# Splitting weights of later stages during the feed-forward stages, with the parts kept in DRAM

## The chip, the cores and the metric

One core of a Trainium2 chip runs the whole program. The metric is the device time of one execution in microseconds (us), and the median of several runs counts. The engines are named as the profile names them: PE multiplies matrices, PEld loads its weights, DVE, ACT and POOL do the elementwise work, and SP issues all the DMA transfers of this kernel.

## The reference, cut to what matters

The program computes a first block of two layers (each: feed-forward 1, a mix of three attentions, feed-forward 2) and a second block (memory attention, forgetting attention "fox", linear recurrence "lru", stick-breaking attention "sb", then a convolved feed-forward), all in float32, for 512 tokens of width 1024.

```python
def hybrid_layer(x, ...):
    x = x + 0.5 * swiglu(rmsnorm(x, ffn1_norm), ffn1_w_gate, ffn1_w_up, ffn1_w_down)
    h = rmsnorm(x, mix_norm) @ w_in
    ...
    x = x + jnp.concatenate([o_a, o_b, o_c], axis=-1) @ w_out
    x = x + 0.5 * swiglu(rmsnorm(x, ffn2_norm), ffn2_w_gate, ffn2_w_up, ffn2_w_down)
    return x
```

`o_b` attends only to the 128 keys with the highest scores of each query; `o_a` and `o_c` are dense. Block 2 projects the normalized state with one wide matrix, runs the four branches, gates them and adds them up.

## The kernel before, in words

**Number format.** PE multiplies in a format (fp32r) that holds only the upper part of a float32. Each weight tile is therefore split into a high part `wh` and a rest `wl`, the activations likewise, and `mm3` (lines 308 to 310) makes three matmuls of them: high by high, high by rest, rest by high. The product of a 128 x 1024 weight tile and 512 tokens is 8 x 3 = 24 matmuls of 128 x 512.

**A weight tile's way.** `weights` (line 283) takes a tile `raw` (two buffers) and loads it by a DMA of SP (line 289). ACT copies it into `wh` (line 293); DVE, for every other tile POOL, subtracts and writes `wl` (line 296). `wh` and `wl` have four buffers each. So a tile costs one load of up to 512 KB, one ACT and one DVE or POOL instruction.

**Stages.** `ffn` (line 392) goes over 22 hidden blocks in two halves (12 and 10): gate and up projections of a block, the gating by ACT, POOL and DVE, a split of the result; then 8 output blocks per half, each with two down tiles of 768 or 640 columns. `mix` (line 594) projects, ropes, and runs 16 heads in the order of `MIX_PLAN`: heads A, C, B; scores and the search for the 128 best keys (`topk`, lines 661 and 662 on DVE) belong to heads B. In `head` (line 463) DVE adds the bias and finds the maximum (473), ACT takes the exponential (478), POOL scales the row (480), PE transposes (517), ACT and DVE split the transposed weights (302, 303), PE multiplies with the values (527). At the end the head outputs are split into `hs` (302, 303) and multiplied with `wo`. `block2` runs `memkv`, then `mem`, `fox`, `lru`, `sb`.

**Order.** The code is written in program order; a scheduler of the language lays every instruction into a fixed queue of its engine ahead of the run, from its own estimate of when operands and buffers come free. Each engine works through its queue in order, SP too: a transfer that waits for a buffer holds up those behind it. Small transfers are in SP's queue as well: the swaps of rope (569, 570) and the copies that stack queries and keys (440, 449).

**Names used.** `st` is a tile of 128 x 1280 with two buffers that holds softmax rows in the attention stages; `nt` is a two-part tile of 128 x 512 with two buffers, used for queries and keys. Neither is used in `ffn` before the change.

## Time and profile before

| | |
|---|---|
| median of 3 runs | 3550.11 us (3547.43 to 3553.41) |
| the profiled execution, its own time | 3547.53 us |
| span in the profile (first to last instruction) | 3545.1 us |
| PE busy | 3452.3 us, 97% |
| DVE, ACT, POOL busy | 1959.9, 1432.8, 1534.5 us (55%, 40%, 43%) |
| mean granted PE clock | 0.988 |
| DMA moved | 397.60 MB, mean 112 GB/s |

Busy time of an engine is the time in which at least one of its instructions ran; PE's is modelled and overlaps from one matmul to the next. The granted clock is the share of PE's full clock: 1.00 is 2.4 GHz, and a stretch at 0.66 was for two thirds of it at 1.2 GHz.

### The profile page before, as it was taken

What the parts mean: (1) busy time and instruction counts of PE and PEld (TensorE: products, weight loads), DVE (VectorE), ACT (ScalarE), POOL (GpSimd) and SP (SyncE); (2) the same over time, 40 slices, a digit from 0 to 9 for tenths busy, and PEclk for the clock granted to TensorE, in tenths of its full rate; (3) what the DMA queues carried; (4) which work ended last, traced back from release to release, by engine and by line L of the source; (5) the groups of instructions that cost most, each with busy time, mean ns of one, the idle gap of its engine ahead of it and who ended that gap; (6) DMA issues with size and microseconds to landing.
All of it is one profiled execution on the core that took longest, in us unless ns stands there. A gap on an engine that the chain in (4) does not pass through costs nothing.

```text
span 3545.1 us, 45441 instructions
## 1 busy us (share of the span) xinstructions
PE 3452.3 (97%) x16648; PEld 2882.8 (81%) x16648; DVE 1959.9 (55%) x3210; ACT 1432.8 (40%) x2366; POOL 1534.5 (43%) x1224
## 2 busy tenths in 40 slices
PE   8999999999999999999999999999999999999999
PEld 7888778788888888777888888888777788888887
DVE  5434697653445344796643465358536655657363
ACT  4223455532333233465422344346525445533222
POOL 3333346342424232446333343258635557635342
PEclk9999999999999999999999999999999999999999
DMA  3333433333233333334433243344532454442332
GB/s 134 91 106 107 128 99 112 109 99 97 94 98 95 95 101 124 110 90 118 122 93 108 85 129 107 104 132 137 152 122 90 157 160 129 128 143 95 95 101 89
DMA packets 141261, 397.60 MB, mean 112 GB/s; under 512 B 18144, under 2 KB 21600, under 8 KB 141040
## 3 DMA queue, kind: packets, MB, share of 16 engines
q1 hardware_dynamic: 141040, 394.71, 36.6%
q8 instruction: 132, 2.16, 0.3%
q14 instruction: 89, 0.73, 0.1%
HBM read 327.24 MB, written 20.48 MB: 98 GB/s over the span
## 4 chain that ended last, share of the span: by engine, by line
PE 47%; DVE 5%; POOL 2%; ACT 2%; issue 2%; DMA 1%; SPq 0%; POOLq 0%; ACTq 0%; DVEq 0%
PE pd L308 10%; PE pd L309 10%; PE pd L310 10%; PE pa L308 4%; PE pa L309 4%; PE pa L310 4%; PE po L527 1%; PE pt L517 1%; DVE wl L296 1%; PE pa L456 1%; POOL st L503 0%; DMA qk<-nt 0%; DVE st L1087 0%; POOL f L499 0%; ACT wh L293 0%
## 5 line engine op out<-in xcount | busy, mean ns | idle before, releaser
L296 POOL TENSOR_TENSOR wl<-raw,wh 128x1024 fp32r<-128x1024 f32 (+3 forms) x315 | 718.0, 2279 | 1135.7 <-ACT wh L293 1112.7
L293 ACT ACTIVATE wh<-raw 128x1024 fp32r<-128x1024 f32 (+3 forms) x631 | 609.5, 967 | 1323.7 <-PE pd L309 841.2
L308 PE MATMUL pd<-hs,wh 128*128 128x512 f32 (+1 forms) x2008 | 791.2, 395 | 19.7 <-ACT wh L293 7.8
L309 PE MATMUL pd<-hs,wh 128*128 128x512 f32 (+1 forms) x2008 | 790.9, 394 | 5.8 <-DVE hs L303 5.4
L310 PE MATMUL pd<-hs,wl 128*128 128x512 f32 (+1 forms) x2008 | 790.5, 394 | 2.4 <-DVE wl L296 1.7
L296 DVE TENSOR_TENSOR wl<-raw,wh 128x1024 fp32r<-128x1024 f32 (+3 forms) x316 | 383.4, 1213 | 232.8 <-ACT wh L293 226.2
L308 PEld LDWEIGHTS pd<-hs,wh 128*128 128x128 f32 (+1 forms) x2008 | 378.4, 189 | 100.7 <-ACT wh L293 14.1
L309 PEld LDWEIGHTS pd<-hs,wh 128*128 128x128 f32 (+1 forms) x2008 | 379.2, 189 | 84.8 <-DVE hs L303 6.2
L310 PEld LDWEIGHTS pd<-hs,wl 128*128 128x128 f32 (+1 forms) x2008 | 378.6, 189 | 85.2 <-DVE wl L296 4.6
L308 PE MATMUL pa<-hs,wh 128*128 128x512 f32 x896 | 349.3, 390 | 0.0
L309 PE MATMUL pa<-hs,wh 128*128 128x512 f32 x896 | 349.2, 390 | 0.0
L310 PE MATMUL pa<-hs,wl 128*128 128x512 f32 x896 | 349.0, 389 | 0.0
L408 POOL TENSOR_TENSOR f<-f,g 128x512 f32<-128x512 f32 x88 | 145.0, 1650 | 279.9 <-ACT g L406 273.5
L407 DVE TENSOR_TENSOR f<-pa,rb 128x512 f32<-128x512 f32 x88 | 60.8, 691 | 272.4 <-PE pa L310 272.4
L310 PEld LDWEIGHTS pa<-hs,wl 128*128 128x128 f32 x896 | 168.4, 188 | 35.0
L309 PEld LDWEIGHTS pa<-hs,wh 128*128 128x128 f32 x896 | 168.2, 188 | 34.9
L308 PEld LDWEIGHTS pa<-hs,wh 128*128 128x128 f32 x896 | 168.4, 188 | 34.6
L480 POOL TENSOR_SCALAR st<-st,ta 128x128 f32<-128x128 f32 x192 | 111.7, 584 | 107.1 <-DVE ta L479 101.0
L303 DVE TENSOR_TENSOR pt<-pt 128x384 fp32r<-128x384 f32 (+1 forms) x200 | 116.8, 597 | 50.0 <-ACT pt L302 48.7
L308 PE MATMUL pd<-ys,wh 128*128 128x512 f32 x362 | 142.3, 393 | 0.2 <-DVE f L741 0.2
L310 PE MATMUL pd<-ys,wl 128*128 128x512 f32 x362 | 141.9, 392 | 0.0
L309 PE MATMUL pd<-ys,wh 128*128 128x512 f32 x362 | 141.8, 392 | 0.0
(385 smaller groups left out, 6468.3 us busy)
## 6 DMA issues: line engine op xcount, KB each, us to landing
raw<-in_wg_dram SPq DMA_DIRECT2D x88, 512.0 KB, 3.5
raw<-in_wu_dram SPq DMA_DIRECT2D x88, 512.0 KB, 3.4
raw<-in_win_dram SPq DMA_DIRECT2D x38, 512.0 KB, 3.5
qk<-nt SPq DMA_DIRECT2D x76, 256.0 KB, 3.9
raw<-in_w2gt_dram SPq DMA_DIRECT2D x32, 512.0 KB, 3.7
raw<-in_w2br_dram SPq DMA_DIRECT2D x32, 512.0 KB, 3.5
qk<-nt SPq DMA_DIRECT2D x108, 128.0 KB, 2.5
raw<-in_wd1a_dram SPq DMA_DIRECT2D x32, 384.0 KB, 3.0
```

The costliest lines, as they stand in the source:

```text
L293: nc.scalar.activation(h[:, :n], raw[:, :n], AF.Copy)
L296: (nc.vector if sub == "v" else nc.gpsimd).tensor_sub(lo[:, :n], raw[:, :n], h[:, :n].bitcast(FT))
L303: (eng or nc.vector).tensor_sub(dst[rows, 1, cols], src, dst[rows, 0, cols].bitcast(FT))
L308: mm(out, wh, xh, start=start, stop=False)
L309: mm(out, wh, xl, start=False, stop=False)
L310: mm(out, wl, xh, start=False, stop=stop)
L407: nc.vector.tensor_mul(u, pu, rb)
L408: nc.gpsimd.tensor_mul(ga, ga, s)
L456: self.nc.tensor.matmul(ps[:, :n], q[:, s, t], k[s][:, x, :n], start=x == 0, stop=x == 1)
L480: nc.gpsimd.tensor_scalar(st[:, c], st[:, c], sm, 0.0, op0=OP.mult, op1=OP.add)
L517: nc.tensor.transpose(pt[:, at + (i - lo) * P:at + (i - lo + 1) * P], st[:, OFF[i] + j * P:OFF[i] + (j + 1) * P], self.ident)
L527: nc.tensor.matmul(po[:, q:q + n], va[:, o:o + P], w[:, x, c:c + n], start=j == 0 and x == 0, stop=j == 2 * g + 1 and x == 1)
```

## The change

During four of the feed-forward stages `prepare` loads tiles of weights that a later stage uses into `st`, splits them in halves of 512 columns into `nt` (ACT copies, DVE subtracts for every other tile, POOL for the rest), and stores both parts into a tile in DRAM. `weights` called with a key loads the two stored parts straight into `wh` and `wl`, with no instruction of ACT, DVE or POOL. The tables: feed-forward 1 of layer 0 prepares 36 tiles of mix 0; feed-forward 2 of layer 0 those of mix 1; feed-forward 1 of layer 1 27 tiles (fox, two of the recurrence); feed-forward 2 of layer 1 40 tiles (recurrence, stick-breaking). That is 139 tiles, in 261 halves. `wo`, the gates and branches of block 2, `mem`, and all feed-forward weights are split as before. Line numbers of the changed kernel are higher: the copy of the split is line 301 and its subtraction 304, the new ones are 324 (load), 330 (copy), 331 (subtraction), 333 (stores), 291 and 292 (loads of the parts).

```diff
-    def weights(self, ap, n):
+    def weights(self, ap, n, key=None):
         nc = self.nc
+        if key in self.ahead:
+            t = self.ahead.pop(key)
+            h = self.wp.tile([P, 1024], FR, name="wh", bufs=4)
+            lo = self.wp.tile([P, 1024], FR, name="wl", bufs=4)
+            nc.sync.dma_start(h[:, :n].bitcast(FT), t[0])
+            nc.sync.dma_start(lo[:, :n].bitcast(FT), t[1])
+            return h, lo
         raw = self.wp.tile([P, 1024], FT, name="raw", bufs=2)
...
+    def prepare(self, share):
+        nc = self.nc
+        self.due += share
+        while self.due >= 1 and self.todo:
+            self.due -= 1
+            name, n, *idx = self.todo.pop(0)
+            ap = self.I[name]
+            for i in idx:
+                ap = ap[i]
+            raw = self.sp.tile([P, 1280], FT, name="st")
+            nc.sync.dma_start(raw[:, :n], ap)
+            d = self.dp.tile([2, P, n], FT, name=f"ah_{name}_{'_'.join(map(str, idx))}")
+            eng = nc.gpsimd if len(self.ahead) % 2 else nc.vector
+            for a in range(0, n, S):
+                m = min(S, n - a)
+                t = self.hl("nt")
+                nc.scalar.activation(t[:, 0, :m], raw[:, a:a + m], AF.Copy)
+                eng.tensor_sub(t[:, 1, :m], raw[:, a:a + m], t[:, 0, :m].bitcast(FT))
+                for x in range(2):
+                    nc.sync.dma_start(d[x][:, a:a + m], t[:, x, :m].bitcast(FT))
+            self.ahead[name, *idx] = d
...
     def ffn(self, f, l):
         nc, I = self.nc, self.I
+        self.todo, self.due = AHEAD.get((f, l), [])[:], 0.0
+        share = len(self.todo) / (2 * KD * (NF - 3) + KD * NF)
...
                 hid.append(t)
+                if n > 2:
+                    self.prepare(2 * KD * share)
...
+                self.prepare((b - a) * share)
+        self.prepare(len(self.todo) + 1)
...
-            wa = [self.weights(I[f"wav_{l}"][g], 768) for g in range(4)]
+            wa = [self.w(f"wav_{l}", 768, g) for g in range(4)]
...
+def _ahead():
+    out = {}
+    for l, at in ((0, (1, 0)), (1, (2, 0))):
+        out[at] = ([(f"win_{l}", D, n) for n in range(19)] + [(f"wav_{l}", 768, g) for g in range(4)]
+                   + [(f"wbv_{l}", 640, g) for g in range(4)] + [(f"wuv_{l}", 640)]
+                   + [(f"wuk_{l}", 256, p) for p in range(3)] + [(f"wuq_{l}", 384, h) for h in range(C_H)])
+    out[1, 1] = ([("w2ff", P)] + [(f"w2f{n}", D, p) for n in "qkv" for p in range(8)] + [("w2la_", D), ("w2lx_", D)])
+    out[2, 1] = [(f"w2l{n}", D, d) for n in "xg" for d in range(8)] + [(f"w2s{n}", D, p) for n in "qkv" for p in range(8)]
+    return out
```

The other call sites change in the same way as the one shown (`self.w(name, n, *index)` in place of `self.weights(I[name][index], n)`).

**How the queues move, first place.** SP, first feed-forward stage, where the down tiles `wd1a` of its first half are loaded. Before, this stretch of the queue is loads of weights alone (the last of the 24 gate and up tiles, then 16 down tiles in one row):

```order
L289 DMA raw<-in_wg_0_dram 128x1024
L289 DMA raw<-in_wu_0_dram 128x1024
L289 DMA raw<-in_wd1a_dram 128x768 x16
L289 DMA raw<-in_wg_0_dram 128x1024
L289 DMA raw<-in_wu_0_dram 128x1024
```

With the change, between two down tiles stand the load of the next tile to prepare and the four stores of an earlier one:

```order
L324 DMA st<-in_wav_dram 128x768
L333 DMA ah_wav_2_2029<-nt 128x512 x2
L333 DMA ah_wav_2_2029<-nt 128x256
L297 DMA raw<-in_wd1a_dram 128x768
L333 DMA ah_wav_2_2029<-nt 128x256
L324 DMA st<-in_wbv_dram 128x640
L333 DMA ah_wav_3_2115<-nt 128x512 x2
L297 DMA raw<-in_wd1a_dram 128x768
L333 DMA ah_wav_3_2115<-nt 128x256 x2
```

In the queue the 36 tiles of this stage do not spread over all of it: 18 loads stand ahead of the last of its first 24 gate and up tiles, 17 more ahead of the last of the 16 down tiles `wd1a`, the last one right behind, and none later. The feed-forward 2 of layer 0 has, counted in the same way, 23 (5 of them ahead of its own weights, among those of `wo`), then 18, then 16 and 6 in its second half, the tiles for fox among them; the feed-forward 1 of layer 1 has none left. The feed-forward 2 of layer 1 has 22, then 12, then 6.

**Second place.** POOL, first mix, the ropes of heads B (`L571`, `L572` before, `L614`, `L615` after). Before:

```order
L571 TENSOR_TENSOR f<-f,x 128x512
L572 TENSOR_TENSOR g<-g,x 128x512
L296 TENSOR_TENSOR wl<-raw,wh 128x1024
L303 TENSOR_TENSOR nt<-f,nt 128x512
L480 TENSOR_SCALAR st<-st,ta 128x128
```

After:

```order
L614 TENSOR_TENSOR f<-f,x 128x512
L615 TENSOR_TENSOR g<-g,x 128x512
L340 TENSOR_TENSOR nt<-f,nt 128x512
L523 TENSOR_SCALAR st<-st,ta 128x128
L523 TENSOR_SCALAR st<-st,ta 128x256
```

The subtractions of the mix's own weights are gone from between the ropes and the scaling of softmax rows; those of `wo` are still there.

**Third place.** ACT, end of the first mix: `pt` is the split of a head's transposed softmax, `fa` the folding of a head's output, and the `hs` are the last head outputs that the multiplication with `wo` waits for. Before:

```order
L302 ACTIVATE pt<-pt 128x384 x2
L535 ACTIVATE fa<-po 64x512
L302 ACTIVATE pt<-pt 128x512
L302 ACTIVATE pt<-pt 128x384
L302 ACTIVATE hs<-ys 128x512
L535 ACTIVATE fa<-po 64x512
L302 ACTIVATE hs<-ys 128x512
```

After:

```order
L339 ACTIVATE pt<-pt 128x384 x2
L578 ACTIVATE fa<-po 64x512
L339 ACTIVATE pt<-pt 128x512
L330 ACTIVATE nt<-st 128x512 x2
L339 ACTIVATE pt<-pt 128x384
L339 ACTIVATE hs<-ys 128x512
L578 ACTIVATE fa<-po 64x512
L339 ACTIVATE hs<-ys 128x512
```

The copies of the first tile that the next feed-forward stage prepares now stand ahead of the last head's last split.

## Rows read from the trace of the kernel before

**Rows 1.** The page, part 1: busy us and share, instructions; PE's clock in 40 slices.
```profile
PE 3452.3 (97%) x16648; PEld 2882.8 (81%) x16648; DVE 1959.9 (55%) x3210; ACT 1432.8 (40%) x2366; POOL 1534.5 (43%) x1224
```

**Rows 2.** Windows: length, busy us (instructions) of each engine, granted clock, DMA share, GB/s.
```profile
100.00:200.00 100.00, 100.00 (x443) 82.84 (x442) 35.66 (x36) 25.43 (x31) 29.25 (x15) 1.00 0.31 95
2820.00:2840.00 20.00, 20.00 (x90) 16.55 (x89) 4.34 (x5) 7.22 (x9) 10.79 (x6) 1.00 0.88 284
```

**Rows 3.** Windows of the first mix, then of the second, where topk runs.
```profile
485.00:500.00 15.00, 15.00 (x83) 13.01 (x82) 14.82 (x40) 6.89 (x16) 6.07 (x9) 1.00 0.29 79
500.00:515.00 15.00, 10.74 (x49) 9.07 (x48) 14.93 (x50) 8.11 (x23) 4.07 (x8) 0.66 0.50 130
515.00:530.00 15.00, 12.91 (x76) 10.89 (x74) 14.81 (x43) 10.19 (x26) 7.42 (x10) 1.00 0.35 96
...
1530.00:1545.00 15.00, 11.67 (x68) 10.54 (x69) 14.27 (x38) 5.98 (x14) 4.56 (x4) 0.91 0.49 122
1545.00:1560.00 15.00, 12.47 (x57) 9.78 (x57) 13.02 (x45) 9.68 (x28) 5.59 (x11) 0.87 0.36 104
```

**Rows 4.** Line 296 in 395:545 and 1440:1560: ns min/median/max, first and last start, forms.
```profile
L296 DVE TENSOR_TENSOR wl<-raw,wh x12: 406/1068/2372, 394.1 to 542.1; 128x1024 fp32r<-128x1024 f32 x5, 128x640 fp32r<-128x640 f32 x3, 128x384 fp32r<-128x384 f32 x2, 128x768 fp32r<-128x768 f32 x1
L296 DVE TENSOR_TENSOR wl<-raw,wh x9: 417/1209/2370, 1447.5 to 1559.4; 128x1024 fp32r<-128x1024 f32 x5, 128x384 fp32r<-128x384 f32 x2, 128x640 fp32r<-128x640 f32 x1, 128x256 fp32r<-128x256 f32 x1
```

**Rows 5.** Windows of both mixes, where heads B begin.
```profile
605.00:620.00 15.00, 10.15 (x42) 8.40 (x43) 12.97 (x27) 5.01 (x15) 9.82 (x10) 0.77 0.32 83
620.00:635.00 15.00, 11.73 (x57) 9.44 (x58) 11.29 (x37) 9.30 (x25) 11.52 (x15) 0.77 0.61 148
...
1650.00:1665.00 15.00, 9.22 (x43) 7.14 (x42) 8.49 (x27) 8.19 (x22) 13.65 (x16) 0.66 0.69 167
```

**Rows 6.** Timelines of POOL, DVE and PE from 602: start, us, instruction [idle before <- releaser].
```profile
603.21 1.29 POOL L303 TENSOR_TENSOR nt<-f,nt 128x512 fp32r<-128x512 f32 x1
604.47 1.25 POOL L571 TENSOR_TENSOR f<-f,x 128x512 f32<-128x512 f32 x1
605.69 1.25 POOL L572 TENSOR_TENSOR g<-g,x 128x512 f32<-128x512 f32 x1
606.91 2.33 POOL L296 TENSOR_TENSOR wl<-raw,wh 128x1024 fp32r<-128x1024 f32 x1
...
602.48 7.31 DVE L303 TENSOR_TENSOR hs<-ys,hs 128x512 fp32r<-128x512 f32 x1
...
609.85 0.79 PE L309 MATMUL pd<-hs,wh 128*128 128x512 f32 x1 [5.41 <-DVE hs L303]
```

**Rows 7.** Waits of PE: us in total, times, longest. First 1560:1680, then 2600:2850.
```profile
PE pt L517 <- POOL st L480: 6.1, 3, 4.1
...
PE pd L308 <- ACT fa L1080: 5.1, 3, 1.8
PE pd L310 <- DVE wl L296: 1.7, 5, 0.4
```

**Rows 8.** Windows in stick-breaking.
```profile
2960.00:2980.00 20.00, 17.82 (x142) 16.88 (x140) 15.16 (x25) 11.54 (x28) 15.53 (x26) 1.00 0.43 107
...
3000.00:3020.00 20.00, 18.88 (x107) 16.19 (x106) 11.89 (x15) 11.26 (x25) 20.00 (x28) 1.00 0.65 167
```

**Rows 9.** Timeline of ACT in the first down stage: copies of two down tiles, one after the other.
```profile
153.39 0.85 ACT L293 ACTIVATE wh<-raw 128x768 fp32r<-128x768 f32 x1 [3.23 <-PE pd L309]
157.47 0.85 ACT L293 ACTIVATE wh<-raw 128x768 fp32r<-128x768 f32 x1 [3.23 <-PE pd L309]
```

**Rows 10.** Page, part 5: groups (x count | busy us, mean ns | idle before); then waits of SP and of PE.
```profile
L296 POOL TENSOR_TENSOR wl<-raw,wh 128x1024 fp32r<-128x1024 f32 (+3 forms) x315 | 718.0, 2279 | 1135.7 <-ACT wh L293 1112.7
L293 ACT ACTIVATE wh<-raw 128x1024 fp32r<-128x1024 f32 (+3 forms) x631 | 609.5, 967 | 1323.7 <-PE pd L309 841.2
...
SPq L289 <- POOL wl L296: 1343.8, 278, 21.2
...
PE pa L456 <- DMA qk<-nt: 2.9, 3, 2.1
```

**Rows 11.** Timelines: prices of 128 x 512 on ACT and DVE; SP's time to issue one load.
```profile
658.14 0.63 ACT L302 ACTIVATE hs<-ys 128x512 fp32r<-128x512 f32 x1 [0.75 <-DVE ys L536]
658.81 0.69 DVE L303 TENSOR_TENSOR hs<-ys,hs 128x512 fp32r<-128x512 f32 x1 [0.70 <-ACT hs L302]
...
18.73 0.33 SPq L289 DMA_DIRECT2D raw<-in_wg_dram  x1
```

**Rows 12.** DMA issues: count, KB each, median us from issue to landing.
```profile
raw<-in_wg_dram SPq DMA_DIRECT2D x88, 512.0 KB, 3.5
...
xd<-x SPq DMA_DIRECT2D x24, 256.0 KB, 2.1
...
gd<-fa SPq DMA_DIRECT2D x14, 256.0 KB, 2.8
```

**Rows 13.** Timeline of PE: its wait in the first stage for the norm's factor.
```profile
36.27 0.50 PE L308 MATMUL pd<-hs,wh 128*128 128x512 f32 x1 [1.74 <-DVE f L405]
```

More of the change, by code (lines that the diff above doesn't have):

```diff
@@ L222, in __init__ @@
         self.spare = True
+        self.ahead, self.todo, self.due = {}, [], 0.0
     def consts(self):
@@ L297, in weights, with w @@
         return h, lo
+    def w(self, name, n, *idx):
+        ap = self.I[name]
+        for i in idx:
+            ap = ap[i]
+        return self.weights(ap, n, (name, *idx))
+    def prepare(self, share):
[4 more added lines that the diff above has]
+            name, n, *idx = self.todo.pop(0)
+            ap = self.I[name]
+            for i in idx:
+                ap = ap[i]
+            raw = self.sp.tile([P, 1280], FT, name="st")
[10 more added lines that the diff above has]
+            self.ahead[name, *idx] = d
     def split(self, dst, src, rows=slice(0, P), cols=slice(0, S), eng=None):
@@ L597, in mix @@
         ci, si, tk = (self.table(k) for k in (2, 3, 4))
-        win = I[f"win_{l}"]
         def tile_of(n):
-            w = self.weights(win[n], D)
+            w = self.w(f"win_{l}", D, n)
             ps = self.ps()
@@ L703, in values_b @@
         def values_b():
-            wb = [self.weights(I[f"wbv_{l}"][g], 640) for g in range(4)]
+            wb = [self.w(f"wbv_{l}", 640, g) for g in range(4)]
             vb.extend(self.hl("v") for _ in range(3))
@@ L902, in vgroup @@
     def vgroup(self, hs, name, grp, rc):
-        w = [self.weights(self.I[name][2 * grp + q], 1024) for q in range(2)]
+        w = [self.w(name, 1024, 2 * grp + q) for q in range(2)]
         vs = [self.hl("v") for _ in range(2)]
@@ L963, in forget @@
         def forget(_):
-            w = self.weights(I["w2ff"], P)
+            w = self.w("w2ff", P)
             pf = self.ps()
@@ L990, in queries @@
         def queries(p):
-            w = self.weights(I["w2fq"][p], D)
+            w = self.w("w2fq", D, p)
             ps = self.ps()
@@ L996, in keys @@
         def keys(p):
-            w = self.weights(I["w2fk"][p], D)
+            w = self.w("w2fk", D, p)
             ps = self.ps()
@@ L1035, in lru @@
         nc, I = self.nc, self.I
-        wa = self.weights(I["w2la_"], D)
-        wx = self.weights(I["w2lx_"], D)
+        wa = self.w("w2la_", D)
+        wx = self.w("w2lx_", D)
         ys = []
@@ L1043, in lru @@
                 d = d0 + e
-                w = self.weights(I["w2lx"][d], D)
+                w = self.w("w2lx", D, d)
                 px = self.ps()
@@ L1100, in queries @@
         def queries(p):
-            w = self.weights(I["w2sq"][p], D)
+            w = self.w("w2sq", D, p)
             ps = self.ps()
@@ L1108, in keys @@
         def keys(p):
-            w = self.weights(I["w2sk"][p], D)
+            w = self.w("w2sk", D, p)
             ps = self.ps()
```

9 lines of the change are left out of this document (5 added, 4 removed).

## The prediction

> **What bounds the kernel now.** I read the page first. PE is busy for 3452.3 of 3545.1 us [rows 1], so all that a change off PE can win is PE's idle 93 us and the stretches where its clock was low; the reader should see there that no other engine is near its limit on average. The averages hide two kinds of stage, so the windows came next. A feed-forward stage has PE at 100.00 of 100 us at clock 1.00, with ACT, DVE and POOL at a quarter to a third and DMA at 95 GB/s [rows 2]: nothing can be won there, and 443 matmuls in 100 us make a weight tile of 24 matmuls last 5.42 us. The idle time lies in the attention stages. While the best keys are searched, DVE is full (14.82 of 15 us), and at the end of that stretch PE stands idle for 4.26 and 2.09 us, in the second mix for 3.33 and 2.53 us [rows 3]. Where heads B begin, PE is idle for 4.85, 3.27 and 5.78 us in windows with clocks of 0.77 and 0.66 [rows 5].
>
> **What it removes.** 36 tiles of each mix and 67 of block 2 lose their copy on ACT and their subtraction, which alternates between DVE and POOL.
>
> *Search stretch.* In it DVE does 12 subtractions of 1.07 us in the middle, 12.8 us, and 9 of 1.21 us, 10.9 us, in the second mix [rows 4]. DVE is what PE waits for here, and both sums are above PE's idle time (6.35 and 5.86 us), so I take all of that idle time as won: 12.2 us. The clock of 0.66 means 10 of 15 us at 1.2 GHz, in which PE lost at most 5 us, most of it already counted as idle; 3 us more for both mixes. Together -15 (bounds 0, if DVE's chain and not its load holds PE, and -20).
>
> *Start of heads B.* The longest wait is a subtraction of `hs` on DVE that takes 7.31 us where the same shape takes 0.69 [rows 6, 11]. All that time POOL runs without a gap, and DVE is through 0.5 us after POOL's run ends with a weight subtraction of 2.33 us. PE waits 5.41 us. So the row shows DVE held up until POOL has nothing ready, and a subtraction taken out of such a run shortens the wait by its 2.33 us. The Trainium skill (SBUF — State Buffer, Who interferes with whom) says that a DVE instruction with two SBUF inputs and a POOL instruction reading SBUF exclude each other, the later one waiting until the other has finished. By that rule DVE would have come in after the first of them, the subtraction at the run's end would cost it nothing, and this stall would give 0; the row shows otherwise, and I go by the row. The second mix waits 6.1 us for POOL's scaling of softmax rows [rows 7], which also stand behind weight subtractions. POOL keeps the ropes and the subtractions of `wo`, so I take half of the 13.9 us, and 2 us for the clock: -9 (0 to -18).
>
> *Block 2.* The recurrence waits 1.7 us directly for `wl` and 5.1 for a bank that DVE and ACT release late [rows 7]; I take the first and half of the second, 4 us. Stick-breaking has POOL at 15.53 and 20.00 of 20 us with PE idle 2.18 and 1.12 us beside it [rows 8], and loses 12 subtractions on POOL: 3 us. Fox waits mostly at its end, where no prepared weight is left: 1 us. Together -8 (-2 to -14). The gains sum to 32.
>
> **What it adds in the feed-forward stages.** 261 halves, each an ACT copy of 0.63 us, a subtraction of 0.69 on DVE or 1.29 on POOL [rows 6, 11], and two stores; 139 loads. On engines that are two thirds idle [rows 2] that costs nothing in itself: the 64 halves of a mix add 40 us to ACT in the 195 us of 24 gate and up and 16 down tiles. Their cover is that nothing in PE's supply has to wait. That supply has a reserve: ACT's weight copy waits for PE to release one of four buffers [rows 9], so it stands three tiles ahead, 12 us in the down stage (one tile per 4.08 us there).
>
> The queue order shows that the tiles are not spread out: 18 are done beside 24 gate and up tiles (7.2 us each) and 18 beside the down tiles, one per 4.08 us. What holds a tile back is `nt`: a buffer is busy for copy, subtraction, two issues of 0.33 and the landing of the store, 2.1 to 2.8 us [rows 11, 12]. That is 4.1 us with DVE and up to 5.4 with POOL, and a tile of two halves needs each of the two buffers once. Ten of the 18 tiles are such, so the lag is 0 to 13 us against a reserve of 12. Transfers: a down tile and a prepared one of the same 393 KB move 4 x 393 KB in 4.08 us, 385 GB/s. The trace's best window moved 284 GB/s at a share of 0.88 [rows 2], which I extend to 323 at full share: 4.87 us a pair, 8 us of lag over ten, within the reserve. Beside gate and up tiles it is 314 GB/s, just under. The Trainium skill (DMA: Bandwidth & Descriptors, Where 436 GB/s comes from) puts the ceiling at 435 GB/s; by that the pair would fit into 4.08 us and this lag would be 0. No run here shows such a rate, so the sum goes by 323. I take +3 for the three preparing stages (0 to +30).
>
> **Waits that it adds or moves.** At each mix's end two copies of the next stage's first tile now stand on ACT ahead of the last head's split: 2 x 0.63 us each, and a load's landing of 3.5 us [rows 12] if it is late; the last `hs` and PE's multiplication with `wo` queue behind. +2.5 for both (0 to +9). At the program's start the first tiles' copies and subtractions stand between the squares of the norm, for whose factor PE already waits 1.74 us [rows 13]: +2 (0 to +5). In the attention stages SP now waits for PE to release `wh` before it loads both parts, and rope swaps and stacking copies queue behind; before, it waited just so, through the subtraction (1343.8 us in total [rows 10]). A freed buffer was refilled by copy and subtraction, 0.97 + 2.28 us with POOL, and now by a landing of 3.5 [rows 10, 12]: even. Loads of a mix grow by 14.5 MB, 45 us of full DMA in some 280 us; PE waits only 2.9 us for transfers today [rows 10], and I add 2 us (0 to +6).
>
> **Sum.** -32 + 3 + 2.5 + 2 + 2 = -22.5. The profiled execution took 3547.5 us (2.4 more than its span), which gives 3525; the median shown is 2.6 us above that execution, so I forecast **3528 us**. What I can call a difference here is 0.2%, 7 us.
>
> **The rivals.**
> *Preparing becomes the bound (slower).* Place: `nt` in the feed-forward stages. If stores land in 5 us instead of 2.1 to 2.8 because DMA runs near its limit, a buffer's round is 7.0 to 7.6 us, 7.3 in the mean. The 18 tiles beside gate and up tiles then just keep pace (7.2 us), but the ten beside down tiles lose 3.2 us each, 32 us, less the reserve of 12: 20 us of PE idle. The feed-forward 2 of layer 0 has nine such tiles beside its first down tiles and six beside the second, at 3.4 us apiece: 17 + 13. The one for block 2 has 12 beside 16 down tiles, 5.4 us each: 10. That is 60 us, and 3528 + 60 - 3 = 3585 us. At a landing of 3 us the reserve is used up; at 4 us the same sums give 10 + 8 + 7 + 0 = 25 us, which takes the whole gain: from there on it decides. For it: 314 GB/s of 323, and SP and ACT work in order, so a late store holds the next weight copy. Against it: the stores that the trace has land in 2.1 to 2.8 us. Chance 0.22, with mishaps of the same sign but smaller among them.
> *No change.* PE's waits in the mixes are links of a chain (maximum, exponential, scaling, transposing) that stays, and the scheduler lays all queues anew; the gains come to a third, 11 us, and the costs of 9.5 eat them: 3549 by the median. For it: the waits are many and short. Against it: DVE at 99% in the search stretch. Chance 0.15.
> *The whole idle time goes.* All bounds of the gains (20 + 18 + 14 = 52) at costs of 5: 3503. For it: the mean clock of 0.988 means 85 us at 1.2 GHz, which would run twice as fast once PE has no gaps. Chance 0.15.
> That the change doesn't do what it says is excluded by the queue: the subtractions are gone from the mixes.
>
> **How the numbers follow.** My forecast's own case has 0.48 and spans 3512 to 3542; with the third rival, faster by over 0.2% has 0.63, the same 0.15, slower 0.22. The range of 8 in 10 is 3500 to 3562: it leaves out half of the slow rival (0.12) and the tail of the best case (0.07).
>
> **What would show it.** In the profile after: feed-forward windows still at PE 100%, with ACT, DVE and POOL higher and DMA at 280 to 320 GB/s in the first 200 us; no PE idle time put down to `wh` or `wl` there. Search windows with DVE under 14 us of 15 and PE full. No DVE instruction stretched to 7 us beside a weight subtraction of POOL. I am wrong if down stages show PE idle with `nt` stores landing in over 4 us, or if the mixes keep their idle 25 us with DVE no longer full.

## The result, and the profile after

The change makes the kernel slower: 3593.6 us (3592.6 to 3596.4) against 3549.5 for the kernel before beside it, a ratio of 1.0126 with a 95% interval of 1.0114 to 1.0139. The forecast of 3528 us (3500 to 3562) was wrong, and on the wrong side; the time came out near that of the rival "preparing becomes the bound" (3585 us).

First the page of the changed kernel (its parts 1 and 4), which answers to [rows 1]:

```profile
PE 3456.5 (96%) x16648; PEld 2886.9 (80%) x16648; DVE 1962.0 (55%) x3271; ACT 1454.9 (41%) x2490; POOL 1521.9 (42%) x1285
...
PE 71%; DMA 12%; DVE 4%; POOL 4%; issue 3%; ACT 3%; SPq 1%; ACTq 0%; POOLq 0%; DVEq 0%
PE pd L345 16%; PE pd L346 16%; PE pd L347 16%; PE pa L345 6%; PE pa L346 6%; PE pa L347 6%; DMA ah_win<-nt 2%; PE po L570 2%; POOL nt L331 2%; PE pt L560 2%; DMA ah_w2lg<-nt 1%; PE pa L499 1%; ACT nt L330 1%; DVE nt L331 1%; DMA ah_w2fk<-n
```

PE is busy about as long as before (3452.3 us), but the span has grown by 46.5 us to 3591.6, so nearly all of the growth, 42.3 us, is idle time of PE. The chain of waits now runs for 12% of the span over transfers (1% before), and the line below names which: `ah_win<-nt`, the stores of the prepared parts, and the copy `nt L330` behind them.

The windows, 100 us each, show where (busy time and instructions of PE, PEld, DVE, ACT and POOL; then the granted clock, the DMA share and GB/s). The first answers to [rows 2]; the kernel before has 100.00 us of PE at clock 1.00 in all these places:

```profile
100.00:200.00 100.00, 89.82 (x381) 72.53 (x380) 46.43 (x50) 38.11 (x61) 47.10 (x31) 0.95 0.86 285
800.00:900.00 100.00, 91.93 (x392) 74.89 (x391) 43.27 (x48) 35.01 (x61) 45.67 (x32) 0.95 0.82 268
900.00:1000.00 100.00, 98.39 (x433) 80.74 (x432) 52.80 (x51) 41.88 (x59) 50.89 (x30) 1.00 0.93 318
1000.00:1100.00 100.00, 89.80 (x377) 72.68 (x376) 58.05 (x60) 43.66 (x66) 40.52 (x25) 0.93 0.72 238
1900.00:2000.00 100.00, 90.27 (x386) 73.62 (x385) 42.47 (x48) 40.66 (x61) 44.05 (x27) 0.95 0.93 321
```

The reader should see three things. PE stands idle for 8 to 10 us in four of the five windows. Its clock falls to 0.93 to 0.95 besides. And no other engine is near its limit: DVE at half, ACT at 35 to 44, POOL at 41 to 51 of 100. Only the DMA share is high.

To say what each stage gained or lost I mark the stages in both traces by DVE's first gating product and its last addition to the residual stream; a scheduler may move matmuls across such a border, and these are counted at 0.2257 us each (443 in 100 us, [rows 2]). Differences of the profiled executions, in us:

| stage | the change | forecast |
|---|---|---|
| feed-forward 1, layer 0 (prepares) | +19.0 | +3 for the three that prepare, +2 for the start |
| mix 0 | -2.9 | -24 for both mixes, +2.5 for their ends, +2 for their loads |
| feed-forward 2, layer 0 (prepares) | +28.8 | |
| feed-forward 1, layer 1 (its tiles were drawn ahead) | 0.0 | 0 |
| mix 1 | +1.2 | |
| feed-forward 2, layer 1 (prepares) | +12.9 | |
| block 2 | -12.5 | -8 |
| all | +46.5 | -22.5 |

So two things went wrong at once: the preparing stages cost 61 us where I had 3, and the mixes gave 2 where I had 24.

What does PE wait for in the preparing stages? Its waits (engine, tile and line, what released it: us in all, times, longest), first the longest for 40 to 400 us, then those for 800 to 1100, then for 1900 to 2000:

```profile
PE pd L345 <- ACT qk L339: 6.8, 1, 6.8
```

```profile
PE pd L345 <- ACT pt L339: 7.8, 1, 7.8
PE pd L345 <- ACT qk L339: 7.1, 1, 7.1
PE pd L345 <- ACT wh L301: 2.6, 2, 1.5
```

```profile
PE pd L345 <- ACT qk L339: 9.7, 1, 9.7
```

One long wait at each of four turns, for the high part of the last hidden tile (L339), where a half of the stage goes over from gate and up tiles to down tiles: 31.4 of the 42 us. For weight copies (`wh`) PE waits little. ACT makes the copy of the hidden tile in well under a microsecond; it is late because ACT is late. And this copy has less to spare than a weight copy. Before the change ACT ends it at 149.21 us in the first half of the first stage, and PE comes to this tile 3.5 us later:

```profile
148.58 0.63 ACT L302 ACTIVATE qk<-f 128x512 fp32r<-128x512 f32 x1 [2.50 <-DVE f L409]
...
152.69 0.39 PE L308 MATMUL pd<-qk,wh 128*128 128x512 f32 x1
```

In the change it begins at 164.47 us, with five copies of prepared halves between it and the hidden split ahead of it; at the three other turns there are four.

ACT's waits tell why it is late, over the first feed-forward stage from 40 to 240 us, first before the change, then after it:

```profile
ACT wh L293 <- PE pd L309: 84.7, 27, 4.3
ACT wh L293 <- PE pa L309: 45.6, 12, 3.9
```

```profile
ACT nt L330 <- DMA ah_win<-nt: 45.1, 19, 5.3
ACT nt L330 <- DMA ah_wbv<-nt: 15.5, 5, 5.2
ACT nt L330 <- DMA ah_wav<-nt: 13.0, 7, 3.2
```

Before, ACT waited 130 us for PE to release a weight buffer: it was ahead, and this waiting is the reserve of three tiles that [rows 9] show. After, none of its waits there is for PE. ACT waits for stores to land before it may write the next prepared half into `nt` (74 us), and the weight copies and hidden splits queue behind. The reserve is gone.

The chain of waits from 104 to 129 us shows the round of a buffer, piece by piece (start, duration, what):

```profile
106.03 0.68 DVE nt L331
...
106.92 4.95 DMA ah_win<-nt
...
111.97 0.64 ACT nt L330
...
112.76 1.27 POOL nt L331
...
114.05 3.28 DMA ah_win<-nt
...
118.81 7.26 DMA ah_win<-nt
```

Subtraction, landing, copy, subtraction, landing: in these 25 us the chain touches neither PE nor the weights of this stage. The landings in it take 3.28 to 7.26 us. In the part of the page on DMA issues the median time to landing is:

```profile
ah_win<-nt SPq DMA_DIRECT2D x152, 256.0 KB, 4.2
st<-in_win_dram SPq DMA_DIRECT2D x38, 512.0 KB, 5.4
```

4.2 us for a store, where I had taken 2.1 to 2.8 from [rows 12]. What sets a landing can be counted from the issues and landings in the traces: such a store has in the median three other transfers of SP's queue under way when it is issued. With two under way it lands in 2.8 us, with four in 4.4, with five in 5.4 (medians of 21, 44 and 16 stores). The kernel before shows the same where it issues in a row: of its 24 stores `xd<-x`, median 2.1 us, the seven with two or more transfers under way land in 3.9 to 4.7.

### The profile page after: what moved, and what is told of

Read it like the earlier page. It is cut to its first block, busy times and chain, and to the rows that moved or that the text cites. A ratio compares the mean times of both kernels' runs of the same rounds, so it can differ in the third digit from the quotient of the medians.

```text
span 3591.6 us, 47953 instructions
## 1 busy us (share of the span) xinstructions
PE 3456.5 (96%) x16648; PEld 2886.9 (80%) x16648; DVE 1962.0 (55%) x3271; ACT 1454.9 (41%) x2490; POOL 1521.9 (42%) x1285
## 4 chain that ended last, share of the span: by engine, by line
PE 71%; DMA 12%; DVE 4%; POOL 4%; issue 3%; ACT 3%; SPq 1%; ACTq 0%; POOLq 0%; DVEq 0%
PE pd L345 16%; PE pd L346 16%; PE pd L347 16%; PE pa L345 6%; PE pa L346 6%; PE pa L347 6%; DMA ah_win<-nt 2%; PE po L570 2%; POOL nt L331 2%; PE pt L560 2%; DMA ah_w2lg<-nt 1%; PE pa L499 1%; ACT nt L330 1%; DVE nt L331 1%; DMA ah_w2fk<-nt 1%
## 5 line engine op out<-in xcount | busy, mean ns | idle before, releaser
L304 POOL TENSOR_TENSOR wl<-raw,wh 128x1024 fp32r<-128x1024 f32 (+2 forms) x246 | 555.9, 2260 | 746.4 <-ACT wh L301 741.6
L301 ACT ACTIVATE wh<-raw 128x1024 fp32r<-128x1024 f32 (+2 forms) x492 | 475.9, 969 | 770.7 <-PE pd L346 453.5
L304 DVE TENSOR_TENSOR wl<-raw,wh 128x1024 fp32r<-128x1024 f32 (+2 forms) x246 | 309.6, 1258 | 248.1 <-ACT wh L301 245.4
L330 ACT ACTIVATE nt<-st 128x512 fp32r<-128x512 f32 (+3 forms) x261 | 153.2, 599 | 354.3 <-DMA ah_win<-nt 83.0
L331 POOL TENSOR_TENSOR nt<-st,nt 128x512 fp32r<-128x512 f32 (+3 forms) x130 | 173.1, 1340 | 215.8 <-ACT nt L330 163.0
L331 DVE TENSOR_TENSOR nt<-st,nt 128x512 fp32r<-128x512 f32 (+3 forms) x131 | 108.5, 840 | 157.1 <-ACT nt L330 133.3
L345 PE MATMUL pd<-ys,wh 128*128 128x512 f32 x362 | 145.0, 400 | 4.1 <-DVE x L461 3.0
```

Source lines behind the costliest of these rows:

```text
L301: nc.scalar.activation(h[:, :n], raw[:, :n], AF.Copy)
L304: (nc.vector if sub == "v" else nc.gpsimd).tensor_sub(lo[:, :n], raw[:, :n], h[:, :n].bitcast(FT))
L330: nc.scalar.activation(t[:, 0, :m], raw[:, a:a + m], AF.Copy)
L331: eng.tensor_sub(t[:, 1, :m], raw[:, a:a + m], t[:, 0, :m].bitcast(FT))
L345: mm(out, wh, xh, start=start, stop=False)
```

## The experiments

The ratio of each run is to the kernel before on the same chip, with its 95% interval. A table at the end of this section has all of them by stage.

**Parts prepared, not used.** The look-up of prepared tiles is taken out; everything else stays.

```diff
-        if key in self.ahead:
+        if key in ():
```

> The tiles are prepared in the feed-forward stages as in the change, but nothing reads the parts: attention loads and splits every weight as the kernel before does. By stage, the changed kernel stands 60 us above the one before in the three preparing stages (18.9 + 28.8 + 12.7) and 14 us below it in the rest (mixes -2, block 2 -12.5). If the loss is the work of preparing alone, and the gain that of the parts alone, this run is 60 us above the kernel before: 3610 us (3602 to 3618). If part of the loss comes from how the parts' loads are queued ahead of the feed-forward stage's first tiles, it is lower: 3585 to 3600.

3602.6 us, 1.0150 (1.0135 to 1.0165), 53 us above the kernel before: within the first expectation, at its low end. By stage the preparing ones lose 51 us (+16.2, +27.7, +7.4), and block 2 is back at the kernel before (+0.5). So the two effects lie apart, with one exception: the mixes, which use nothing here, lose 8.7 us (+6.4 and +2.3, the second within the scatter of a stage). That is where preparing reaches back into the stage ahead of it. In the changed kernel, at the end of mix 0, the chain shows how (the pieces of PE's matmuls left out):

```profile
659.58 3.61 DMA st<-in_win_dram
663.21 0.64 ACT nt L330
...
664.81 4.87 DMA ah_win<-nt
...
670.32 0.61 ACT nt L330
670.94 0.95 ACT wh L301
...
674.01 0.69 DVE x L423
...
674.74 0.79 PE pd L345
...
679.37 0.43 PE pd L346
...
680.17 0.23 PE pd L345
```

The load of the next stage's first prepared tile, which starts as soon as the last softmax rows have left `st`, its copy, the store, the next copy, and only then ACT's copy of a `wo` tile (670.94), the subtraction, the addition to `x`, and PE, which waits 3.7 us. When it resumes, its matmuls take 0.43 us until 680.17 and 0.23 from there: that lower clock costs another 2.5 us.

**Parts used, not prepared.** Only one tile is prepared; all 139 tiles of attention load both parts from it.

```diff
-        self.todo, self.due = AHEAD.get((f, l), [])[:], 0.0
+        self.todo, self.due = AHEAD[1, 0][:1] if (f, l) == (1, 0) else [], 0.0
...
-        if key in self.ahead:
-            t = self.ahead.pop(key)
+        if key in PARTS:
+            t = self.ahead["win_0", 0]
```

> Only one tile is prepared; each of the 139 tiles of attention loads both its parts from that one tile in DRAM, so the attention stages have the loads of the change, and no copy and no subtraction for these weights, while the feed-forward stages prepare nothing (the weights multiplied are therefore those of one tile). If gain and loss lie apart as the stages show, this is 14 us below the kernel before: 3536 us (3530 to 3542). If the preparing stages' own traffic also spoils the attention stages that follow, the gain is larger, up to the 32 us forecast: 3517 to 3528.

3518.9 us, 0.9912 (0.9898 to 0.9927): 30 us gained, not 14, so the first expectation was too small and the second right. Without the preparing the kernel gains nearly what the sum had for the attention stages, 32 us. A second time, beside the next run:

> The run that loads both parts from one prepared tile again, beside the next one with more rounds: 3519 us (3514 to 3523).

3519.1 us, 0.9917 (0.9904 to 0.9931). By stage these two runs have mixes at -13.3 and -19.4, block 2 at -14.5 and -12.3: less in the mixes than the 24 forecast, more in block 2 than the 8.

**One load instead of two.** What is left of the mixes' gain might go to the doubled loads:

```diff
-            lo = self.wp.tile([P, 1024], FR, name="wl", bufs=4)
+            lo = h
...
-            nc.sync.dma_start(lo[:, :n].bitcast(FT), t[1])
```

> As the run that loads both parts from one prepared tile, but only one part is loaded and stands for both (the multiplication with the low part uses the high one), so attention moves half the bytes for these weights. That run was 30 us below the kernel before, with mixes -13, where 24 were forecast. Theory T (the doubled loads eat the rest of the mixes' gain): 3504 to 3512 us. Theory C (what is left in the mixes is the chain of search and softmax, with loads hidden): within 4 us of that run, 3515 to 3523 us.

3513.0 us, 0.9906 (0.9890 to 0.9923): between the two expectations. Once more, on the same chip as the repeated run with both loads:

> The run with one load for both parts again, beside the former, whose medians lay 6 us apart with intervals that overlap, while the profiled executions lay 16 us apart. Theory T (the doubled loads take some of the gain): 6 us or more below the run with both loads. Theory C (loads are hidden): within 4 us of it.

3517.0 us, 0.9912 (0.9900 to 0.9925): 2 us below, with intervals that overlap. PE's idle time in the mixes does fall (from 16.7 and 16.0 us to 11.7 and 12.0), but the time of the stages does not follow (-12.0 and -8.7 against -10.6 and -8.8). So the 45 us of extra DMA time per mix are hidden, to within what these runs can tell.

**More buffers for preparing.** The prepared halves go through tiles of the tags `pt` (four) and `qk` (five), which the feed-forward stage leaves idle in one of its halves, instead of the two `nt`.

```diff
-                t = self.hl("nt")
+                t = self.hl(self.spot)
...
+                self.spot = ("pt", "qk")[half]
```

> The parts wait for their stores in tiles of the feed-forward stage's own idle tags, four or five buffers where the change has two. Theory A (the round of two buffers with a store that lands in 4 to 5 us holds the copies on ScalarE, and the split of the last hidden tile stands behind them): the 42 us of idle TensorE in the preparing stages go and the 18 us of low clock with them, 3536 to 3552 us. Theory B (the DMA engines are at their limit, loads of down tiles come late): unchanged within 10 us, 3583 to 3600 us, with waits of TensorE moved from hidden splits to weights.

3545.2 us, 0.9993 (0.9984 to 1.0003): within the range of theory A. Of the 61 us in the preparing stages 46 are gone, with the same bytes in the whole program, and with stores that land later than in the change (`ah_win<-pt` here, 5.5 us):

```profile
ah_win<-pt SPq DMA_DIRECT2D x136, 256.0 KB, 5.5
```

```profile
100.00:200.00 100.00, 99.43 (x438) 81.54 (x437) 42.77 (x46) 35.08 (x50) 39.62 (x25) 1.00 0.65 216
800.00:900.00 100.00, 100.00 (x443) 82.81 (x442) 34.76 (x40) 31.76 (x49) 35.91 (x25) 1.00 0.61 201
```

PE is full again in windows that had 90 and 92 us. But the run does not change the buffers alone. With other buffers the scheduler laid the work otherwise: beside the first 16 down tiles stand 5 loads of tiles to prepare where the change has 17, the tiles for fox are back in their own stage (50 halves in feed-forward 1 of layer 1, 47 instead of 101 in the stage ahead of it), no prepared copy stands between the last two hidden splits of any half, and the two windows move less (216 and 201 GB/s against 285 and 268). So the run shows that preparing costs little in this order and with these buffers, and does not tell the one from the other. Theory B it does exclude, by a window of the same run: from 60 to 100 us the transfers run at 360 GB/s, where the change has 319, and PE is full.

```profile
60.00:100.00 40.00, 40.00 (x178) 33.14 (x177) 22.44 (x24) 18.26 (x27) 26.34 (x16) 1.00 1.00 360
```

**A gap ahead of the turn.** PE's long waits stand where a half turns to its down tiles. If only that place mattered, it would help to prepare nothing there:

```diff
-                if n > 2:
+                if 2 < n < b - 3:
```

(The share is raised so that as many tiles are prepared.)

> No tile is prepared at the last three hidden tiles of each half; the same number of tiles is spread over the remaining steps. Theory A1 (only the place matters: the split of the last hidden tile stands behind copies that wait): TensorE's waits for the hidden split, 7 to 10 us at four places, go: 3548 to 3565 us. Theory A2 (the lag of the two buffers is carried along whatever stands there, and the denser steps add to it): 3583 to 3610 us.

3591.6 us, 1.0114 (1.0094 to 1.0134), the stages as in the change (+18.1, +28.1, +13.6). The time lies in the range of A2, but the run tests neither theory: the traces show the same instructions in the same order on ACT, POOL and SP as in the change, with the same five and four prepared copies ahead of the last hidden splits. The scheduler lays the queues by when buffers come free, and the gap in the program made no gap in them. The run is a second measurement of the change. What the other runs have to say of the place speaks for A1: in the change, in the run that uses no part and in the one without stores (next), PE waits 4.1 to 9.7 us wherever four to six prepared copies stand between the last two hidden splits of a half; where none to two stand, in the run with more buffers and in the one spread out, it does not wait there. Whether ACT's lag from further ahead would cost without them was not tried.

**No stores.** The same clumped preparing, but only the first tile is stored.

```diff
-                for x in range(2):
+                for x in range(0 if self.ahead else 2):
```

> The change with its clumped order and two buffers, but only the first prepared tile is stored; the others are loaded, copied and subtracted and not stored, and attention loads all parts from that one tile. A buffer is free as soon as its two instructions are through, 1.3 to 1.9 us. If the landing of the stores is what holds the copies on ScalarE: the loss in the preparing stages goes, 3518 to 3532 us. If the loads of the raw tiles or the copies and subtractions themselves hold the feed-forward stage: 3555 us or more.

3561.6 us, 1.0038 (1.0024 to 1.0052): in the range of the second expectation, so stores are not needed for a loss. But the preparing stages lose 30 us (+9.0, +17.4, +3.4), half of the 61. ACT's waits in 720 to 900 us show what takes the stores' place:

```profile
ACT nt L330 <- DMA st<-in_w2fq_dram: 12.1, 8, 3.2
```

The scheduler, with the buffers free at once, draws the halves together still more (21 weight copies stand between the first and the last of the 64 halves of the first stage, where the change has 37), and ACT then stands in front of the loads of the raw tiles, which have two buffers as well. Six prepared copies stand ahead of the last hidden split in the first half of feed-forward 2 of layer 0, and PE waits 8.4 us for it. So the copies wait for the landing of a raw tile if not for that of a store; how much of the 61 us belongs to the stores stays open, since the order changed too.

**Spread out.** Each copy of a prepared half is tied on ACT behind the weight copy that stands ahead of it in the program. Still two buffers, the same tiles, the same bytes:

```diff
-            nc.scalar.activation(h[:, :n], raw[:, :n], AF.Copy)
+            self.mark = nc.scalar.activation(h[:, :n], raw[:, :n], AF.Copy).ins
...
-                nc.scalar.activation(t[:, 0, :m], raw[:, a:a + m], AF.Copy)
+                with self.tc.issue_after(self.mark):
+                    nc.scalar.activation(t[:, 0, :m], raw[:, a:a + m], AF.Copy)
```

In ACT's queue 68 weight copies then stand between the first and the last of the 64 halves of the first stage, where the change has 37, and the tiles for fox are back in their own stage.

> The change with its two buffers, but each copy of a prepared tile is queued on ScalarE behind the weight copy ahead of it in the program, so that the halves are spread over all 78 to 84 weight tiles of four feed-forward stages where the scheduler had drawn them into the first 40 of three (and 53 of them a whole stage ahead). Theory P (the scheduler's clumping asks for a half per 2.7 us, which two buffers at 3 us per half can't give; spread, it is one per 4.5 us or more): the loss in the feed-forward stages goes, 3519 to 3530 us. Theory B2 (every copy that stands on ScalarE behind a store holds the weight copies, however they are spread): 3545 to 3575 us.

3534.1 us, 0.9966 (0.9953 to 0.9978): faster than the kernel before by 0.34%, and 4 us above the range of theory P. The preparing stages are back near the kernel before (+6.4, +0.2, 0.0 and +1.8). Two of the windows above, and the same two views:

```profile
100.00:200.00 100.00, 100.00 (x443) 82.81 (x442) 51.97 (x49) 37.11 (x53) 47.65 (x28) 1.00 0.79 267
...
1900.00:2000.00 100.00, 100.00 (x443) 82.81 (x442) 58.72 (x58) 44.18 (x63) 56.57 (x30) 1.00 0.86 299
```

```profile
ACT wh L301 <- PE pd L347: 32.4, 14, 3.3
ACT wh L301 <- PE pa L347: 27.9, 8, 3.9
...
ACT nt L331 <- DMA ah_win<-nt: 14.0, 7, 4.2
```

```profile
ah_win<-nt SPq DMA_DIRECT2D x152, 256.0 KB, 2.5
```

ACT waits for PE again (60 us in this stretch), PE is full at clock 1.00, and the same stores land in 2.5 us, with two other transfers under way in the median. That is the landing that I had taken from the kernel before; it held for transfers spread out, not for the clump. This is the run that shows the cause as far as it is shown: with the same tiles, bytes and two buffers, and up to 299 GB/s in these windows, an edit of the order of the copies on ACT, with what the scheduler made of it in the other queues, takes back 52 of the 61 us. It moves the copies away from each other and from the turns at once (one or two stand there now), so it does not say which of the two counts.

**Spread out, with more buffers.**

> The same spread, with the four and five buffers of the earlier run besides. By theory P buffers no longer matter: within 4 us of the run with two buffers, 3517 to 3530 us. By theory B2 it is 15 us or more below it, and near the run with buffers alone (3545 us) or better.

3542.3 us, 0.9987 (0.9978 to 0.9997): buffers do not help any more, as theory P has it, but the run is 8 us slower than with two, which neither theory expected. By stage it stands worse at feed-forward 2 of layer 1 and in block 2 (+5.9 and -3.6, against +1.8 and -6.6), but single executions scatter as much. Whether block 2 is late because it starts by asking for `pt` and `qk` was not tried, and the 8 us stay open.

**Spread further.** The first stage starts preparing later, 13 tiles move from the last preparing stage to the one ahead of it, and each stage is done earlier:

```diff
-        share = len(self.todo) / (2 * KD * (NF - 3) + KD * NF)
+        first = 5 if (f, l) == (1, 0) else 2
+        share = 1.15 * len(self.todo) / (2 * KD * (NF - 1 - first) + KD * NF)
...
-                if n > 2:
+                if n > first:
...
+    out[1, 1] += out[2, 1][:13]
+    out[2, 1] = out[2, 1][13:]
```

> The paced version, with three more edits: in the first stage nothing is prepared before the sixth hidden tile instead of the third, 13 of the 40 tiles prepared in the last preparing stage go to the stage before it (which then has 40 and the last one 27), and the shares are 15% larger, so that the last tiles of a stage have none. The paced run stands 6 us above the kernel before in the first stage and has about 7 us more of idle TensorE in the 60 us around the start of block 2. If both come from preparing there, they go: 3522 us (3516 to 3529). If the start is late because of the loads' order, and block 2's start because of its own norm, it is unchanged: 3530 to 3538 us.

3524.8 us, 0.9929 (0.9917 to 0.9942), within the first expectation: the fastest version with all parts prepared, 0.7% under the kernel before and within 6 us of the runs that prepare nothing. It is ahead of both kernels.

**With `wo` as well.** Where heads B begin, PE waits longest for POOL's scaling of softmax rows. First the spread version's wait there (598 to 632 us), then that of the version with `wo` (590 to 700 us):

```profile
PE pt L562 <- POOL st L525: 5.3, 1, 5.3
```

```profile
PE pd L346 <- ACT hs L340: 2.1, 1, 2.1
...
PE pt L562 <- POOL st L525: 0.5, 1, 0.5
```

> The spread version, with the eight tiles of `wo` of each mix prepared as well (44 tiles in each of the two stages ahead of a mix). Where heads B begin, TensorE there waits 5.3 us for GpSimd's scaling of a softmax row, which stands behind a subtraction of `wo` of 2.38 us. If those subtractions hold the scaling: up to 2.4 us less at that wait in each mix, and DVE's part of `wo` beside, 3516 to 3521 us. If GpSimd's ropes hold it, or the larger share takes it back in the feed-forward stages: 3522 to 3530 us.

3534.4 us, 0.9966 (0.9955 to 0.9978): slower than without `wo`, and above both expectations. The wait itself was read rightly, 5.3 us became 0.5, but mix 0 did not get shorter (-5.7 against -7.3); other waits stand there now (`hs` 2.1 us). And the preparing stages, with 80 halves each ahead of the mixes, lose 14 us.

All runs by stage, in us against the profiled execution of the kernel before, worked out as above (ff is a feed-forward stage; first the layer 0 pair around mix 0, then those around mix 1):

| run | ff 1, 0 | mix 0 | ff 2, 0 | ff 1, 1 | mix 1 | ff 2, 1 | block 2 |
|---|---|---|---|---|---|---|---|
| the change | +19.0 | -2.9 | +28.8 | 0.0 | +1.2 | +12.9 | -12.5 |
| parts not used | +16.2 | +6.4 | +27.7 | -0.1 | +2.3 | +7.4 | +0.5 |
| not prepared | +3.1 | -8.5 | +0.4 | -0.1 | -4.8 | +0.1 | -14.5 |
| not prepared, again | +2.8 | -10.6 | 0.0 | 0.0 | -8.8 | -0.1 | -12.3 |
| one load | +0.6 | -12.9 | +0.2 | -0.1 | -9.2 | -0.2 | -20.2 |
| one load, again | +6.5 | -12.0 | +0.4 | +0.1 | -8.7 | 0.0 | -11.9 |
| buffers | +5.1 | -5.4 | +0.2 | +0.1 | -0.5 | +9.3 | -9.5 |
| gap | +18.1 | -2.9 | +28.1 | 0.0 | +0.7 | +13.6 | -11.7 |
| no stores | +9.0 | -6.2 | +17.4 | -0.1 | +1.7 | +3.4 | -14.3 |
| spread | +6.4 | -8.4 | +0.2 | 0.0 | -5.9 | +1.8 | -6.6 |
| spread, buffers | +5.8 | -8.3 | 0.0 | -0.1 | -5.6 | +5.9 | -3.6 |
| spread further | +2.0 | -7.3 | +0.2 | +1.5 | -9.4 | -0.1 | -8.5 |
| with `wo` | +9.4 | -5.7 | +4.2 | 0.0 | -6.0 | +0.1 | -11.5 |

Each is one profiled execution: the repeated runs show that a stage can differ by up to 6 us, block 2 by 8, with nothing changed; the gap, whose queues are those of the change, lies within 1 us of it in every stage.

## Why the prediction was wrong, point by point

**The feed-forward stages: the step that failed.** The term that failed is the +3 for the preparing stages, which measured 61. The prediction found the right queue (the tiles are not spread out) and the right place (`nt`), and then went wrong twice. It took "the landing of the store, 2.1 to 2.8 us" from [rows 12]: medians of stores that mostly had one other transfer under way. In the clump three were under way and the store landed in 4.2 us, the sign of being wrong that the prediction had named; in the spread run two, and 2.5. And it set the lag against a reserve of 12 us, which is that of the weight copies; what PE waited for was the split of the last hidden tile, in the same queue behind the same copies, with some 3.5 us to spare. Both were to be read from the trace before: the landings of stores issued in a row, and the 3.5 us. The Trainium skill (DMA: Bandwidth & Descriptors, Latency and other measured facts) says that the confirmation from memory makes up most of a transfer's fixed cost and takes longer the more loaded the memory is. The traces go the same way from 2.5 to 4.2 us for the same stores, but with more buffers the landing is 5.5 us at a lower DMA share (0.65); they show it to grow with the transfers under way at issue, and do not separate the memory's answer from the transfers ahead.

The rival had the mechanism, and its working by stage, 20, 30 and 10 us, stands beside 19.0, 28.8 and 12.9 measured. But that is partly luck: it got there with a landing of 5 us and with the same reserve of 12; at the measured 4.2 its own sums give about 31 (12 + 10 + 8 + 1). What it left out are the turns, the raw tiles' loads, which hold ACT in the same way (the run without stores still loses 30), and the clock, since of the 61 us only 42 are idle time of PE (12.6 in the first stage above the 9.9 of before, 19.9, 9.7) and the rest is work at a lower clock. Its condition, that from a landing of 4 us on it decides, was borne out; a chance of 0.22 for it was too low for a queue that I had seen to be clumped.

**DMA as the limit.** I had extended the best window to 323 GB/s at full share. The changed kernel moves 321 GB/s over a whole 100 us at a share of 0.93, and 386 over the 15 us from 680, above my ceiling. The highest rate here is in the run with more buffers (366 GB/s over the 100 us from 655, and over 20 us of these):

```profile
663.00:683.00 20.00, 19.18 (x84) 15.31 (x83) 12.27 (x14) 10.51 (x16) 7.50 (x5) 1.00 1.04 409
```

So that ceiling was too low, and PE full at 360 GB/s shows that the rate was not what held it. The Trainium skill (DMA: Bandwidth & Descriptors, Where 436 GB/s comes from) has the 435 GB/s that I weighed against it as the ceiling of the fabric, and about 358 as the limit between HBM and SBUF, where these transfers run. 366 and 409 GB/s lie between the two, so here the measurement decides against the lower one.

**The attention stages: a sum that came out, partly by luck.** -32 was forecast; the two runs that prepare nothing are 30 and 29 us faster as a whole. By place it was less right: the mixes gain 13 and 19 us where I had 24, and block 2 gains 14 and 12 where I had 8. In the mixes the gain does not come as idle time: mix 0, as a window before and in the second run without preparing, has

```profile
374.60:707.90 333.30, 314.75 (x1630) 262.24 (x1629) 254.36 (x601) 176.12 (x372) 154.10 (x143) 0.96 0.38 110
```

```profile
377.30:699.90 322.60, 305.90 (x1630) 257.31 (x1629) 224.35 (x585) 152.71 (x339) 116.23 (x126) 0.97 0.49 153
```

the same 1630 matmuls, and idle time of 18.6 and 16.7 us; but PE's busy time falls from 314.75 to 305.90, in part because its clock is up for longer. DVE does 30 us less. In the search stretch I took all 6.35 us of PE's idle time as won, because 12 subtractions took 12.8 us of DVE. But these lie in 150 us, and only three of them, 1.6 us, in the 45 us of [rows 3] (window 485 to 530):

```profile
L296 DVE TENSOR_TENSOR wl<-raw,wh x3: 406/542/627, 493.2 to 524.9; 128x384 fp32r<-128x384 f32 x2, 128x256 fp32r<-128x256 f32 x1
```

And 1.5 us of idle time went: without the preparing DVE is still full in the first of the two windows, and PE still idle for 4.9 us of these 30:

```profile
495.00:510.00 15.00, 12.15 (x69) 10.15 (x69) 14.90 (x43) 6.72 (x17) 4.47 (x6) 0.97 0.53 142
510.00:525.00 15.00, 13.00 (x73) 11.06 (x73) 13.27 (x49) 10.35 (x30) 5.99 (x11) 0.92 0.52 147
```

Where heads B begin, the stretched subtraction of `hs`, 7.31 us, is gone, as forecast, but not for the reason that I gave. It is gone as well in the run that prepares and does not use the parts, which keeps the subtractions of weights in the mix. There POOL works without a gap from 623.66 to 637.8 us, and the subtraction of `hs` that falls into this run takes 0.95 us:

```profile
623.66 1.30 POOL L614 TENSOR_TENSOR f<-f,x 128x512 f32<-128x512 f32 x1 [0.63 <-DMA g<-f]
...
629.79 2.40 POOL L304 TENSOR_TENSOR wl<-raw,wh 128x1024 fp32r<-128x1024 f32 x1
...
624.55 0.95 DVE L340 TENSOR_TENSOR hs<-ys,hs 128x512 fp32r<-128x512 f32 x1
```

So in this run DVE is not held up until POOL has nothing ready; the rule of the Trainium skill that I had set aside (SBUF — State Buffer, Who interferes with whom), by which it waits for one instruction of POOL, is nearer to this row. What stretched the one subtraction to 7.31 us stays open. In the version spread further POOL's scaling holds PE in its place, 5.3 us, as the half that I left standing.

**The mixes' ends.** +2.5 us was forecast, from two copies of ACT. The run that prepares and uses nothing loses 8.7 in the mixes, and the chain at 659 to 674 us shows why: not the copies cost but the landings between them. That is within the bounds that I gave (0 to +9, for a load that is late), and near their end. In the change it took a good part of what the mixes had won.

**What held.** The engines other than PE have room for the work in the feed-forward stages; the extra loads in attention cost next to nothing (2 us, not told apart from 0); the tiles of block 2 gained somewhat more than forecast.

**What would have been right.** With the halves spread over the stages, the time is 3524.8 us, close to the 3528 forecast. By place it is near as well: the mixes gain 17 us where the sum has 19.5 with their costs, block 2 gains 8.5 where it has 8, and the preparing stages with the start lose 4 where it has 5. That the mixes came so near is in part luck, for the gain was not where I had put it. The sum described a change in which the work lies evenly beside other work, and the queue order already said that it did not.

## What to carry to other kernels

Work moved into idle engines is free only as long as nothing it waits for stands in the queue of an engine that feeds the bound: count the buffers of the new work, and the time for which each is held, before counting its instructions. Then look for the instruction of that queue with the least to spare, here the split of the last hidden tile with 3.5 us, and not for the average one. Such work has to be tied to the pace of the stage that carries it, because a scheduler that sees a free engine will draw it together, and an edit of the program's order may not reach the queues at all (the gap): read the queues of a run before reading its time. The spread cost one dependency and turned +1.3% into -0.7% together with a better division over the stages. And the landing time of a transfer belongs to the transfers that are under way when it is issued: when a change issues them in bunches, take it from the bunches in the trace, or let the range reach to what twice that landing does.

## What the runs showed of the hardware

The same 256 KB stores land in 2.5 us when spread (DMA share 0.79 in the window from 100 to 200 us), 4.2 us clumped (0.86), and 5.5 us with more buffers (0.65). So the share does not order them; the number of other transfers of the queue under way at issue does, in the median two, three and five. With the same number the three runs are near each other: with two under way 2.5, 2.8 and 2.8 us. A later landing need not cost more: with more buffers, and another order, the preparing stages lose 15 us at 5.5, with two 61 at 4.2.

After the wait of 3.7 us at the end of mix 0 PE's matmuls of 512 columns take 0.43 us instead of 0.23 for 5.4 us (674.74 to 680.17 in the chain above), the lower of its two levels. In the preparing stages of the change this and idle time go together: 42 us idle, 19 us of slower work.
